# A macaron decoder layer on one core: 512-column products grouped ahead of 256-column ones, and the statistics of two norm boundaries taken another way

## The chip, the core and the metric

The kernel runs on one core of a Trainium2 chip. TensorE multiplies (PE in the rows, with its weight loads as PEld), VectorE (DVE), ScalarE (ACT) and GpSimd (POOL) do the elementwise work, and SyncE (SP) issues nearly all DMAs. The metric is the device time of one execution in microseconds; three executions of the kernel before gave 2088.93, 2089.51 and 2091.53 us, the median being 2089.51.

## The reference

The layer works on 16 meta tokens and 256 tokens (272 in all) of width 2048, in float32:

```
hs = concat(meta, x)                                   # 272 x 2048
f  = swiglu(rms(hs, g1pre), w_gate, w_up, w_down)      # 2048 -> 5632 -> 2048
hs = hs + 0.5 * rms(f, g1post)                         # boundary 1 ...
m  = mixer(rms(hs, g2pre), w_in, ..., w_out)           # ... with this norm
hs = hs + rms(m, g2post)                               # boundary 2 ...
f  = swiglu(rms(hs, g3pre), w_gate2, w_up2, w_down2)   # ... with this norm
out = (hs + 0.5 * rms(f, g3post))[16:]
```

The mixer is one projection by `w_in` (2048 x 7264), two kinds of attention on its parts (top-k attention with an indexer, and gated linear attention), and `w_out` (2048 x 2048). `rms(y, g)` is `y * rsqrt(mean(y*y) + eps) * g`.

## The kernel before, in words

**Products.** Activations lie transposed: 128 features on the partitions, tokens along the free dimension, 16 chunks of 128 features. Each float32 operand is split into an upper part (`hi`, float32r) and the rest (`lo`), and a product is `hi*hi + lo*hi + hi*lo`, summed in PSUM. A weight block of 512 x 512 is loaded by one DMA of 1 MB into a `raw` tile (3 buffers, L110, L220, and L598), and `split` (L103) makes of each half a `whi` tile on ScalarE (L104) and a `wlo` tile on VectorE (L105), 5 buffers each.

**`stream_block` (L144).** One block of 512 output features: 4 units of 512 input features (`u`), in each unit 4 tiles of 128 output features (`f`), and for each of them 4 chunks (`k`). With 272 tokens a chunk takes three products of 272 columns (`mm3`, L137 to L139). With 256 tokens the upper and lower parts of the activation lie side by side, so that a chunk takes one product of 512 columns (`hi` weight by both parts, L192) and one of 256 columns (`lo` weight by the upper part, L193), in turn: 512, 256, 512, 256, and so on. These blocks are 5 blocks of `w_in`, 4 of `w_out`, and 20 of the second gate and up: 29 blocks of 16 times 4 pairs, 1856 pairs. The two halves of the 512 columns are added after it by `joined` (L204: a ScalarE copy of one half, L207, and a VectorE sum, L208).

**`stream_pair` (L210).** Right behind each boundary two blocks run side by side, all in products of 256 columns (L249, L250, L252; at boundary 1 with one more tile of 272 columns): 16 chunks in turn, each with 24 or 27 products. Its weights come as splits numbered `i = 4u + 2j + ...` (L228), four to a unit.

**Operands in SBUF.** `xg` (L275) holds the normed activations of 272 tokens, one chunk to 2 x 272 columns (2176 bytes); `xn2` (L278) is a view of the same tile for 256 tokens, one chunk to 2 x 256 columns (2048 bytes), from its first byte on. `xs2` hands it to `w_out`, and to the second gate and up, as the moving operand.

**The two boundaries.** Boundary 1 lies between the last down projection of the first FFN (`down1`, L570, its last call at L594) and the `w_in` pair; boundary 2 between `w_out` (L1003) and the pair of the second gate and up. Each needs the sum of squares of a whole row before the next stage can start. `square_add` (L337) squares a chunk on ScalarE and adds it on GpSimd, chunk by chunk; the last chunk (15) is squared and added on VectorE (L340, L341). Then `stat_cols` (L292) sums over the partitions on TensorE with a column of ones, `rstd_cols` (L299) makes the reciprocal root (L305 to L310), `Boundary` (L351) spreads it over the partitions with TensorE (`bcast`, L316) and makes the first three chunks of the next stage's activation (`chunk`, L370: VectorE L373 and L376, ScalarE L379 for the upper and VectorE L380 for the lower part); the others follow while `stream_pair` runs. `keep_busy(n)` (L268) puts `n` products of 256 columns with no use for their result into TensorE's queue; the counts stand in `BUSY` (L33): 12 ahead of the statistics, 7 ahead of the spreading, 12 behind it.

**What sets the order.** TensorE's instructions run in the order written. The other engines' order is made by a planner from dependencies and program order; `order(ins, prior)` (L96) tells it to put one instruction behind another on its engine without a wait. `Boundary.how` (L364) puts the splits `i >= 5` of a pair behind chunk 1's upper part on ScalarE; the splits 0 to 4 are free. Behind `down1` (L596 to L604) the kernel loads 96 narrow columns of `w_in` (`small_w`) and splits them, through one of the `raw` buffers.

## Time and profile before

| | |
|---|---|
| three executions | 2088.93, 2089.51, 2091.53 us |
| the profiled execution | 2088.96 us, of which the span from first to last instruction is 2087.2 us |
| TensorE busy | 99% of the span, 13,992 products |
| VectorE, ScalarE, GpSimd busy | 60%, 45%, 2% |
| granted TensorE clock | 0.998 of full speed over the span |
| DMA | 360.72 MB, mean 173 GB/s |

Products are pipelined: the time that the profile gives to one (400 ns for 512 columns) overlaps with that of its neighbours, so the pace is read from the starts of consecutive products. A row of a timeline gives start, duration, engine, line, operation, output and inputs, shape and count.

### The profile page before, as it was taken

The numbers are of one execution on the slowest core, as the hardware profiler recorded it, in microseconds if no ns is written. First come the engines' busy times: TensorE is split into PE (matmuls) and PEld (weight loads), VectorE is DVE, ScalarE is ACT, GpSimd is POOL, SyncE is SP. The second block draws the span as 40 slices with busy tenths as digits, with TensorE's granted clock in tenths as the row PEclk, the third lists the DMA queues.
The fourth block names the chain that finished last, engine by engine and source line by source line (L and its number), as shares of the span: only waits on it lengthen the run. The fifth ranks groups of instructions, "written<-read, shape, count | busy, mean of one in ns | idle before, by whom it ended". The sixth has DMA issues, their size and how long they took to land.

```text
span 2087.2 us, 33405 instructions
## 1 busy us (share of the span) xinstructions
PE 2066.7 (99%) x13992; PEld 1922.0 (92%) x13992; DVE 1260.7 (60%) x1874; ACT 944.2 (45%) x1348; POOL 50.1 (2%) x64
## 2 busy tenths in 40 slices
PE   9999999999999999999999999999999999999998
PEld 9999999999999999989989998898888888888886
DVE  6455555545555557778755454766656565566657
ACT  6333333333343345564544355564444444444443
POOL 3000000000000002000000001100000000000000
PEclk9999999999999999999999999999999999999999
DMA  7555555555555555444443445465655555555653
GB/s 246 172 172 183 168 176 181 166 179 178 168 180 177 168 181 152 151 141 140 161 140 123 159 145 179 145 202 183 196 186 182 193 190 183 191 191 183 198 184 121
DMA packets 184649, 360.72 MB, mean 173 GB/s; under 512 B 9919, under 2 KB 10513, under 8 KB 184354
## 3 DMA queue, kind: packets, MB, share of 16 engines
q1 hardware_dynamic: 183552, 356.41, 52.4%
q8 instruction: 110, 1.80, 0.4%
q10 hardware_dynamic: 786, 2.14, 0.3%
q14 instruction: 41, 0.34, 0.1%
q0 software_dynamic: 160, 0.03, 0.0%
HBM read 356.46 MB, written 2.10 MB: 172 GB/s over the span
## 4 chain that ended last, share of the span: by engine, by line
PE 97%; DVE 2%; ACT 1%; issue 1%; DMA 0%; POOL 0%; SPq 0%; DVEq 0%; ACTq 0%
PE mmb L192 21%; PE mmb L139 15%; PE mmb L137 15%; PE mmb L138 15%; PE mmb L193 10%; PE mmb L1039 4%; PE mmb L1040 4%; PE mmb L1041 4%; PE mmb L249 2%; PE mmb L250 2%; PE mmb L252 2%; PE axb L790 1%; PE axb L855 0%; DVE wlo L105 0%; PE axb L704 0%
## 5 line engine op out<-in xcount | busy, mean ns | idle before, releaser
L105 DVE TENSOR_TENSOR wlo<-raw,whi 128x1024 fp32r<-128x1024 f32 (+1 forms) x674 | 807.1, 1221 | 608.0 <-ACT whi L104 607.9
L104 ACT ACTIVATE whi<-raw 128x1024 fp32r<-128x1024 f32 (+1 forms) x674 | 684.2, 1050 | 809.5 <-PE mmb L139 408.8
L192 PE MATMUL mmb<-xg,whi 128*128 128x512 f32 x1856 | 661.5, 400 | 0.0
L193 PE MATMUL mmb<-xg,wlo 128*128 128x256 f32 x1856 | 521.1, 281 | 0.0
L137 PE MATMUL mmb<-xg,whi 128*128 128x272 f32 x1792 | 520.5, 290 | 0.2 <-DVE qk L631 0.2
L139 PE MATMUL mmb<-xg,whi 128*128 128x272 f32 x1792 | 517.4, 289 | 0.0
L138 PE MATMUL mmb<-xg,wlo 128*128 128x272 f32 x1792 | 514.8, 287 | 0.0
L192 PEld LDWEIGHTS mmb<-xg,whi 128*128 128x128 f32 x1856 | 348.8, 188 | 87.3 <-issue 4.0
L193 PEld LDWEIGHTS mmb<-xg,wlo 128*128 128x128 f32 x1856 | 350.5, 189 | 0.4
L137 PEld LDWEIGHTS mmb<-xg,whi 128*128 128x128 f32 x1792 | 336.6, 188 | 4.9 <-issue 3.6
L139 PEld LDWEIGHTS mmb<-xg,whi 128*128 128x128 f32 x1792 | 337.5, 188 | 0.0
L138 PEld LDWEIGHTS mmb<-xg,wlo 128*128 128x128 f32 x1792 | 336.8, 188 | 0.2
L139 PE MATMUL mmb<-hlo,whi 128*128 128x272 f32 x704 | 204.1, 290 | 0.0
L137 PE MATMUL mmb<-hhi,whi 128*128 128x272 f32 x704 | 203.8, 289 | 0.0
L138 PE MATMUL mmb<-hhi,wlo 128*128 128x272 f32 x704 | 202.1, 287 | 0.0
L1039 PE MATMUL mmb<-whi,hhi 128*128 128x512 f32 (+1 forms) x356 | 138.0, 388 | 0.0
L1041 PE MATMUL mmb<-wlo,hhi 128*128 128x512 f32 (+1 forms) x356 | 137.8, 387 | 0.0
L1040 PE MATMUL mmb<-whi,hlo 128*128 128x512 f32 (+1 forms) x356 | 137.7, 387 | 0.0
L137 PEld LDWEIGHTS mmb<-hhi,whi 128*128 128x128 f32 x704 | 133.1, 189 | 0.0
L139 PEld LDWEIGHTS mmb<-hlo,whi 128*128 128x128 f32 x704 | 132.7, 188 | 0.0
L138 PEld LDWEIGHTS mmb<-hhi,wlo 128*128 128x128 f32 x704 | 132.5, 188 | 0.0
L583 DVE TENSOR_TENSOR acc<-mmb,acc 128x272 f32<-128x272 f32 x160 | 70.0, 439 | 78.0 <-PE mmb L139 78.0
(262 smaller groups left out, 1634.9 us busy)
## 6 DMA issues: line engine op xcount, KB each, us to landing
raw<-in_ffn_w_up_dram SPq DMA_DIRECT2D x88, 1024.0 KB, 5.1
raw<-in_ffn_w_down_dram SPq DMA_DIRECT2D x88, 1024.0 KB, 5.0
raw<-in_ffn_w_gate_dram SPq DMA_DIRECT2D x87, 1024.0 KB, 5.1
raw<-in_w_in_dram SPq DMA_DIRECT2D x56, 1024.0 KB, 5.0
raw<-in_w_out_dram SPq DMA_DIRECT2D x16, 1024.0 KB, 5.0
xn<-in_x_dram SPq DMA_DIRECT2D x3, 512.0 KB, 8.1
raw<-in_ffn_w_gate_dram SPq DMA_DIRECT2D x4, 256.0 KB, 5.1
grep<-in_ffn_post_g_dram ACTq DMA_DIRECT2D x1, 1024.0 KB, 4.9
```

The source lines that it names most:

```text
L104: for ins, prior in zip((act.activation(hi, raw, AF.Copy), eng.tensor_tensor(lo, raw, hi.bitcast(F32), op=ALU.subtract)), after):
L105: eng.tensor_tensor(lo, raw, hi.bitcast(F32), op=ALU.subtract)), after):
L137: pe.matmul(ps, whi, xhi, start=start, stop=False)
L138: pe.matmul(ps, wlo, xhi, start=False, stop=False)
L139: pe.matmul(ps, whi, xlo, start=False, stop=stop)
L192: pe.matmul(wide, hi, both, start=ui == 0 and k == 0, stop=False)
L193: pe.matmul(wide[:, 0], lo, both[:, 0], start=False, stop=ui == 3 and k == 3)
L249: pe.matmul(ps, hi, xh, start=c == 0 and own, stop=False, skip_group_check=True)
L583: dve.tensor_tensor(acc[:, c], ps[:, :T], acc[:, c], op=ALU.add)
L1039: pe.matmul(ps, hh[:, tk], whi, start=k == 0, stop=False)
L1040: pe.matmul(ps, hl[:, tk], whi, start=False, stop=False)
L1041: pe.matmul(ps, hh[:, tk], wlo, start=False, stop=k == 3)
```

## The change

Six things change, and the diff below is cut to them.

- In `stream_block` with 256 tokens, the four products of 512 columns of a tile `f` come first and then its four of 256 columns. A tile named in `plain` takes three products of 256 columns for each chunk instead (`mm3`), so that its sum stands in one half of the bank; this is used for the last tile of `w_out` (4 times 4 chunks), whose result is then copied by VectorE without `joined`.
- `xn2` starts `XOFF = 64` elements (256 bytes) into `xg`.
- Squares are added on VectorE for all chunks (before: GpSimd). Chunk 15's square is made on VectorE (`square_last`) but not added there: `stat_cols2` lets TensorE sum the running sum's columns and then the last square's columns into the same place.
- The idle products at the boundaries: 2 (between the two halves of `stat_cols2`), 5 and 9 in place of 12, 7 and 12.
- In `Boundary.how` the lower part of split 0 goes behind the last square, that of split 1 behind the reciprocal, splits 2 to 4 behind chunk 1's upper part (ScalarE) and lower part (VectorE); from 5 on as before.
- The load and split of `small_w` move ahead of the last `gate_up` of the first FFN.

```diff
-BUSY = (12, 2, 12, 7, 12)
+BUSY = (12, 2, 2, 5, 9)
...
+                    x = [xs(4 * u + k)[:, :, sl] for k in range(4)]
                     for k in range(4):
                         hi, lo = wof(k, f)
-                        both = xs(4 * u + k)[:, :, sl]
-                        pe.matmul(wide, hi, both, start=ui == 0 and k == 0, stop=False)
-                        pe.matmul(wide[:, 0], lo, both[:, 0], start=False, stop=ui == 3 and k == 3)
+                        if f in plain:
+                            mm3(wide[:, 0], hi, lo, x[k][:, 0], x[k][:, 1], ui == 0 and k == 0, ui == 3 and k == 3)
+                        else:
+                            pe.matmul(wide, hi, x[k], start=ui == 0 and k == 0, stop=False)
+                    for k in range(0 if f in plain else 4):
+                        pe.matmul(wide[:, 0], wof(k, f)[1], x[k][:, 0], start=False, stop=ui == 3 and k == 3)
...
-    xn2 = xg.rearrange("p c s t -> p (c s t)")[:, :KC * 2 * NX].rearrange("p (c s t) -> p c s t", c=KC, s=2)
+    xn2 = xg.rearrange("p c s t -> p (c s t)")[:, XOFF:XOFF + KC * 2 * NX]
+    xn2 = xn2.rearrange("p (c s t) -> p c s t", c=KC, s=2)
...
+    def stat_cols2(sq, last, toks):
+
+        ps = ax_bank()
+        for j, s in enumerate((sq, last)):
+            for i, (t0, t1) in enumerate(toks):
+                pe.matmul(ps[:, i:i + 1], s[:, t0:t0 + P], ones, start=j == 0 and i == 0, stop=j == 1,
+                          skip_group_check=True)
+            if j == 0:
+                keep_busy(BUSY[2])
+        return ps[:, 0:len(toks)]
...
+    def square_last(src, n):
+        q = st.tile([P, T], F32, name="sqt", bufs=3)
+        return q, dve.tensor_tensor(q[:, :n], src, src, op=ALU.mult)
...
         def how(self, i):
-            return dict(after=(self.later, None)) if i >= 5 else {}
+            if i < 2:
+                return dict(after=(None, self.behind[i]))
+            return dict(after=(self.later, self.lower if i < 5 else None))
...
     for b in range(NB):
+        if b == NB - 1:
+
+            w_in = a["w_in"]
+            small_w = mixp.tile([P, 2, KC, P], F32R, name="mix")
...
     rr1 = st.tile([P, 3], F32, name="rrc", bufs=2)
-    keep_busy(BUSY[2])
-    rstd_cols(rr1, stat_cols(sq, TOK), D, unscaled=ev1)
+    lastq, last = square_last(acc[:, KC - 1], T)
+    root = rstd_cols(rr1, stat_cols2(sq, lastq, TOK), D, unscaled=ev1)
     keep_busy(BUSY[3])
...
             for f in range(4):
                 c = 4 * j + f
-                joined(mix[:, c], banks[f])
-                square_add(sq, mix[:, c], c == 0, NX, last=c == KC - 1)
+                if c < KC - 1:
+                    joined(mix[:, c], banks[f])
+                    prior = square_add(sq, mix[:, c], c == 0, NX)
+        dve.tensor_copy(mix[:, KC - 1], banks[3][:, :NX])
         rr2 = st.tile([P, 3], F32, name="rrc", bufs=2)
-        keep_busy(BUSY[2])
-        rstd_cols(rr2, stat_cols(sq, TOKX), D)
+        lastq, last = square_last(mix[:, KC - 1], NX)
+        order(last, prior)
+        root = rstd_cols(rr2, stat_cols2(sq, lastq, TOKX), D)
```

## Rows read from the trace of the kernel before

**Rows 1.** From the page: busy time and share of the span of each engine, and the chain that ended last by engine.

```profile
PE 2066.7 (99%) x13992; PEld 1922.0 (92%) x13992; DVE 1260.7 (60%) x1874; ACT 944.2 (45%) x1348; POOL 50.1 (2%) x64
PE 97%; DVE 2%; ACT 1%; issue 1%; DMA 0%; POOL 0%; SPq 0%; DVEq 0%; ACTq 0%
```

**Rows 2.** From the page: the costliest groups of instructions, here the split on VectorE and the 512-column products (count, busy us, mean ns of one, idle before).

```profile
L105 DVE TENSOR_TENSOR wlo<-raw,whi 128x1024 fp32r<-128x1024 f32 (+1 forms) x674 | 807.1, 1221 | 608.0 <-ACT whi L104 607.9
...
L192 PE MATMUL mmb<-xg,whi 128*128 128x512 f32 x1856 | 661.5, 400 | 0.0
```

**Rows 3.** TensorE's timeline in the second FFN: the first product of two blocks of gate and up (128 pairs), the first of the 96 products of 512 columns of the down projection behind them, and the first product behind that.

```profile
1452.33 0.39 PE L192 MATMUL mmb<-xg,whi 128*128 128x512 f32 x1
...
1497.54 0.40 PE L1039 MATMUL mmb<-whi,hhi 128*128 128x512 f32 x1
...
1519.37 0.39 PE L192 MATMUL mmb<-xg,whi 128*128 128x512 f32 x1
```

**Rows 4.** The same timeline: the 5th and the 12th of those 96 products.

```profile
1498.49 0.39 PE L1040 MATMUL mmb<-whi,hlo 128*128 128x512 f32 x1
...
1500.10 0.39 PE L1041 MATMUL mmb<-wlo,hhi 128*128 128x512 f32 x1
```

**Rows 5.** From the chain that ended last, in order of time (start, us, what): the last 8 products of a chunk of the pair behind boundary 2, and those of the chunk 12 chunks later; a chunk is 24 products of 256 columns.

```profile
1340.02 0.96 PE mmb L252 x8
...
1374.58 0.96 PE mmb L252 x8
```

**Rows 6.** TensorE's timeline in the pair behind boundary 1: first and last of 16 products of 256 columns in chunk 1, and of the same 16 in chunk 2.

```profile
824.55 0.29 PE L249 MATMUL mmb<-xg,whi 128*128 128x256 f32 x1
...
826.26 0.28 PE L250 MATMUL mmb<-xg,wlo 128*128 128x256 f32 x1
...
827.70 0.28 PE L249 MATMUL mmb<-xg,whi 128*128 128x256 f32 x1
...
829.47 0.28 PE L250 MATMUL mmb<-xg,wlo 128*128 128x256 f32 x1
```

**Rows 7.** Boundary 1, timeline of TensorE: the last product of the down projection, the statistics, and the first product of the pair.

```profile
811.64 0.29 PE L139 MATMUL mmb<-hlo,whi 128*128 128x272 f32 x1
...
815.82 0.83 PE L296 MATMUL axb<-ones,sq 128*128 128x1 f32 x6 [2.47 <-DVE sq L341]
...
821.00 0.41 PE L249 MATMUL mmb<-xg,whi 128*128 128x256 f32 x1
```

**Rows 8.** Boundary 1, timeline of VectorE and, last, of ScalarE.

```profile
811.96 0.44 DVE L583 TENSOR_TENSOR acc<-mmb,acc 128x272 f32<-128x272 f32 x1 [1.06 <-PE mmb L139]
812.40 1.52 DVE L105 TENSOR_TENSOR wlo<-raw,whi 128x1024 fp32r<-128x1024 f32 x1
813.85 0.43 DVE L340 TENSOR_TENSOR sqt<-acc 128x272 f32<-128x272 f32 x1
814.20 1.21 DVE L105 TENSOR_TENSOR wlo<-raw,whi 128x1024 fp32r<-128x1024 f32 x1
815.34 0.43 DVE L341 TENSOR_TENSOR sq<-sq,sqt 128x272 f32<-128x272 f32 x1
816.69 0.16 DVE L308 SCALAR_TENSOR_TENSOR pv<-axb,ev 128x3 f32<-128x3 f32 x1 [0.92 <-PE axb L296]
817.12 0.18 DVE L310 RECIPROCAL rrc<-sd 128x3 f32<-128x3 f32 x1 [0.27 <-ACT sd L309]
818.67 0.44 DVE L373 TENSOR_TENSOR bu<-acc,axb 128x272 f32<-128x272 f32 x1 [1.38 <-PE axb L321]
...
819.68 0.52 ACT L379 ACTIVATE xg<-hsT,gcol 128x272 fp32r<-128x272 f32 x1 [2.59 <-DVE hsT L376]
```

**Rows 9.** Busy time of each engine in stretches of boundary 1 (window, its length, busy us and count of PE, PEld, DVE, ACT, POOL, then the granted clock, DMA share and GB/s).

```profile
814.00:816.00 2.00, 0.18 (x2) 0.18 (x2) 1.77 (x3) 0.00 (x0) 0.00 (x0) 1.00 0.73 179
...
820.00:822.00 2.00, 2.00 (x12) 2.00 (x12) 1.97 (x5) 1.36 (x4) 0.00 (x0) 0.56 0.03 8
```

**Rows 10.** Boundary 2, timeline of TensorE: the last product of `w_out` and the first of the pair.

```profile
1327.01 0.28 PE L193 MATMUL mmb<-xg,wlo 128*128 128x256 f32 x1
...
1334.97 0.39 PE L249 MATMUL mmb<-xg,whi 128*128 128x256 f32 x1
```

**Rows 11.** Boundary 2, timeline of VectorE, with the ScalarE square of chunk 14 first.

```profile
1327.47 0.40 ACT L346 ACTIVATE sqt<-mix 128x256 f32<-128x256 f32 x1
...
1328.74 0.42 DVE L208 TENSOR_TENSOR mix<-mmb,sqt 128x256 f32<-128x256 f32 x1
1329.12 1.37 DVE L105 TENSOR_TENSOR wlo<-raw,whi 128x1024 fp32r<-128x1024 f32 x1
1330.42 0.41 DVE L340 TENSOR_TENSOR sqt<-mix 128x256 f32<-128x256 f32 x1
1330.93 0.42 DVE L341 TENSOR_TENSOR sq<-sq,sqt 128x256 f32<-128x256 f32 x1
1332.35 0.17 DVE L310 RECIPROCAL rrc<-sd 128x2 f32<-128x2 f32 x1 [0.99 <-ACT sd L305]
1333.43 0.42 DVE L373 TENSOR_TENSOR bu<-mix,axb 128x256 f32<-128x256 f32 x1 [0.92 <-PE axb L321]
```

**Rows 12.** SyncE's issue of the load of `small_w`; and, from the page, the loads of a weight matrix with KB each and median us from issue to landing.

```profile
790.36 1.76 SPq L601 DMA_DIRECT2D raw<-in_w_in_dram  x2
...
raw<-in_ffn_w_up_dram SPq DMA_DIRECT2D x88, 1024.0 KB, 5.1
```

More of the change, by code (lines that the diff above doesn't have):

```diff
@@ L144, in stream_block @@
     def stream_block(w, c0, xs, sl, korder=(0, 1, 2, 3), chunked=False, extra=None, before=None, how=None,
-                     raw=None):
+                     raw=None, plain=()):
         n = sl.stop - sl.start
@@ L309, in rstd_cols @@
             act.activation(q[:, :w], v[:, :w], AF.Sqrt)
-        dve.reciprocal(dst[:, :w], q[:, :w])
+        return dve.reciprocal(dst[:, :w], q[:, :w])
     def eps_var(dst, src, n):
@@ L335, in sqrt_table, with square_add @@
         act.activation(j, after, AF.Sqrt, bias=eps, scale=0.0)
-    def square_add(sq, src, first, n, eng=pool, last=False):
-        if last:
-            q = st.tile([P, T], F32, name="sqt", bufs=3)
-            dve.tensor_tensor(q[:, :n], src, src, op=ALU.mult)
-            dve.tensor_tensor(sq[:, :n], sq[:, :n], q[:, :n], op=ALU.add)
-        elif first:
+    def square_add(sq, src, first, n):
+        if first:
             act.activation(sq[:, :n], src, AF.Square)
@@ L379, in chunk @@
             h = act.activation(hi, hsT[:, c, sl], AF.Copy, scale=gn[:, c:c + 1])
-            dve.scalar_tensor_tensor(lo, hsT[:, c, sl], gn[:, c:c + 1], hi.bitcast(F32),
-                                     op0=ALU.mult, op1=ALU.subtract)
+            i = dve.scalar_tensor_tensor(lo, hsT[:, c, sl], gn[:, c:c + 1], hi.bitcast(F32),
+                                         op0=ALU.mult, op1=ALU.subtract)
             if c == 1:
-                self.later = h
+                self.later, self.lower = h, i
         def __call__(self, ui, k):
@@ L399, in __call__ @@
                 for d in range(c, c + 1) if c < 12 else range(12, KC):
-                    self.last = square_add(self.sq, hsT[:, d, self.sl], d == 0, self.n, dve)
+                    self.last = square_add(self.sq, hsT[:, d, self.sl], d == 0, self.n)
     grow = const.tile([P, P], F32, name="grow")
@@ L583, in down1 @@
                     dve.tensor_tensor(acc[:, c], ps[:, :T], acc[:, c], op=ALU.add)
-                if b == NB - 1:
-                    square_add(sq, acc[:, c], c == 0, T, last=c == KC - 1)
+                if b == NB - 1 and c < KC - 1:
+                    square_add(sq, acc[:, c], c == 0, T)
                 bg.tick(12 * us)
@@ L589, in layer_kernel @@
     for b in range(NB):
+        if b == NB - 1:
+            w_in = a["w_in"]
+            small_w = mixp.tile([P, 2, KC, P], F32R, name="mix")
+            raw = wp.tile([P, KC, P], F32, name="raw", bufs=3)
+            pool.memset(raw[:, :, 64:128], 0.0)
+            for c0, n, o in ((C_IK, 80, 0), (C_GL, 16, 96)):
+                nc.sync.dma_start(out=raw[:, :, o:o + n],
+                                  in_=w_in[:, c0:c0 + n].rearrange("(k p) c -> p k c", p=P))
+            for j in range(2):
+                js = slice(8 * j, 8 * j + 8)
+                split(raw[:, js], small_w[:, 0, js], small_w[:, 1, js])
         hid = gate_up(fp, a["ffn1_w_gate"], a["ffn1_w_up"], b, xs, full, begin.r, first if b == 0 else None)
@@ L594, in layer_kernel @@
     down1(NB - 1, prev)
-    w_in = a["w_in"]
-    small_w = mixp.tile([P, 2, KC, P], F32R, name="mix")
-    raw = wp.tile([P, KC, P], F32, name="raw", bufs=3)
-    pool.memset(raw[:, :, 64:128], 0.0)
-    for c0, n, o in ((C_IK, 80, 0), (C_GL, 16, 96)):
-        nc.sync.dma_start(out=raw[:, :, o:o + n], in_=w_in[:, c0:c0 + n].rearrange("(k p) c -> p k c", p=P))
-    for j in range(2):
-        js = slice(8 * j, 8 * j + 8)
-        split(raw[:, js], small_w[:, 0, js], small_w[:, 1, js])
     rr1 = st.tile([P, 3], F32, name="rrc", bufs=2)
-    keep_busy(BUSY[2])
-    rstd_cols(rr1, stat_cols(sq, TOK), D, unscaled=ev1)
+    lastq, last = square_last(acc[:, KC - 1], T)
+    root = rstd_cols(rr1, stat_cols2(sq, lastq, TOK), D, unscaled=ev1)
     keep_busy(BUSY[3])
-    bound = Boundary(lambda c: acc[:, c], rr1, TOK, full, g1post, g2pre, r2c, None, xs, full)
+    bound = Boundary(lambda c: acc[:, c], rr1, TOK, full, g1post, g2pre, r2c, None, xs, full, (last, root))
     ffn1_ctx.close()
@@ L1004, in layer_kernel @@
         for j in range(4):
-            banks = stream_block(a["w_out"], j * BW, xs2, alone, korder=korder, before=split_mix if j == 0 else None)
+            banks = stream_block(a["w_out"], j * BW, xs2, alone, korder=korder, before=split_mix if j == 0 else None,
+                                 plain=(3,) if j == 3 else ())
             if j == 2:
@@ L1009, in layer_kernel @@
                 c = 4 * j + f
[L1010 to L1011 removed]
+                if c < KC - 1:
+                    joined(mix[:, c], banks[f])
+                    prior = square_add(sq, mix[:, c], c == 0, NX)
+        dve.tensor_copy(mix[:, KC - 1], banks[3][:, :NX])
         rr2 = st.tile([P, 3], F32, name="rrc", bufs=2)
[L1013 to L1014 removed]
+        lastq, last = square_last(mix[:, KC - 1], NX)
+        order(last, prior)
+        root = rstd_cols(rr2, stat_cols2(sq, lastq, TOKX), D)
         keep_busy(BUSY[3])
[L1016 removed]
+        bound = Boundary(lambda c: mix[:, c], rr2, TOKX, xsl, g2post, g3pre, r3c, ev3, xs2, alone,
+                         (last, root))
         first = stream_pair(a["ffn2_w_gate"], 0, a["ffn2_w_up"], 0, xs2, alone, bound, bound.how)
```

8 lines of the change are left out of this document (4 added, 4 removed).

## The prediction

> **What bounds the kernel now.** I read the page's busy shares and its chain by engine first, then TensorE's timeline in a long stretch without stalls, then all engines' timelines at the two boundaries. The first two give the frame: TensorE is busy 99% of the span and makes up 97% of the chain that ended last [rows 1]. So only two things can shorten the time: a closer pace of its products, or less time at the boundaries, where its queue holds idle products that count as busy.
>
> The pace is read from starts. Two blocks of gate and up, 128 pairs, take 1497.54 - 1452.33 = 45.21 us [rows 3], 353.2 ns a pair. Alone, the two kinds are quicker: from the 12th product of the down projection to the next block's first are 85 products of 512 columns in 1519.37 - 1500.10 = 19.27 us [rows 3, 4], 226.7 ns each; and 12 chunks of 24 products of 256 columns take 1374.58 - 1340.02 = 34.56 us [rows 5], 120.0 ns each. Together 346.7, so a pair taken in turn costs 6.5 ns more than its parts. I read that as a price of changing the length, 3.25 ns a change, two changes a pair.
>
> At boundary 1 the next stage's first product starts 821.00 - 811.64 = 9.36 us after the last one of the stage before [rows 7], at boundary 2 1334.97 - 1327.01 = 7.96 us after it [rows 10]. What ends last there is VectorE's queue: two splits of 1.52 and 1.21 us stand between the sum into chunk 15, its square and its addition [rows 8]; at boundary 2 one of 1.37 us [rows 11]. Both belong to the next stage's weights and could wait.
>
> **The change part by part.** The sum is made against the profiled execution: 2088.96 us, 0.55 below the median of 2089.51; it transfers to the median as a difference.
>
> *Products regrouped.* 1856 pairs [rows 2] are 464 groups of four; four of them become `plain`, 460 change. A group costs 4 x 353.2 = 1413 ns now. Regrouped it has four of each kind and two changes in place of eight: 4 x 346.7 + 2 x 3.25 = 1393 ns, 20 ns less; 460 x 20 = 9.2 us. The trace has no such group, so both ends: the good one has all 512-column products at 226.7 and the 256-column ones at the best pace of the trace, (826.26 - 824.55) / 15 = 114.0 ns [rows 6]: 1363 ns, 23 us less. The bad one takes the nearest rows for a few 512-column products right behind 256-column ones, the first four of the down projection: (1498.49 - 1497.54) / 4 = 237.5 ns [rows 3, 4], with 120.0 for the others: 1430 ns, 7.8 us more. I take 9.2, since the long runs stand on 85 and 288 products, and the four slow ones on one place where weights and bank change as well. I apply it to the 80 groups of `w_in` too, for which I show no row.
>
> *The 256 bytes.* The address of the moving operand does matter in this trace: 16 products take 1.71 us between first and last in chunk 1 and 1.77 us in chunk 2 [rows 6], 114 against 118 ns, and what differs is a step of 2176 bytes in `xg`, which is 8.5 times 256. Whether a step of 256 bytes alone does anything, no row shows; if it repeats the pace at a whole number of 256, it does nothing, and that is the nearest reading. I take 0; ends: 6 ns on 768 products of the second pair, 4.6 us either way.
>
> [...]
>
> *`plain`.* Four groups of twelve 256-column products, 1440 ns in place of 1413: 0.1 us in all, and only the last, at most 0.03 us, meets the boundary. It saves ScalarE's copy of chunk 15. VectorE's copy I price as its sum, 0.42 [rows 11].
>
> *Boundary 1.* VectorE goes from the sum (811.96, done 812.40) straight to the square: done 812.83. The addition is TensorE's now, and the earlier chunks' columns are summed before it. From the end of the last addition (815.77) to the next VectorE step (816.69) are 0.92 us [rows 8], so that step could start at 813.75. But split 0's lower part, 1.22 us [rows 2], is now released by the square and fills the gap till 814.05. Then the reciprocal 0.43 later, 814.48. From it to the spread factor 1.55 us [rows 8], of which I cut 0.15 because seven idle products stood in between and there are five: 815.9. Split 1's lower part, behind the reciprocal, ends at 815.9 as well and costs nothing more. Then 1.01 us to the upper part of chunk 0 and its 0.52 [rows 8]: first product at 817.45 in place of 821.00, 3.55 us less. [...] In sum 3.9.
>
> *Boundary 2.* The copy of chunk 15 and chunk 14's addition, now VectorE's (0.42 each), follow the last product: chunk 14's chain had its square at 1327.47 although a split stood ahead of it [rows 11], so that both are done at about 1328.2, and the square at 1328.6. From the start of the addition to the reciprocal were 1332.35 - 1330.93 = 1.42 us [rows 11], 1.0 without the addition: 1329.6, held by split 0 till 1329.85. The factor 1.08 later [rows 11], 1330.93, held by split 1 (from 1330.0) till 1331.25. From there to the first product 1334.97 - 1333.43 = 1.54 [rows 10, 11]: 1332.8, 2.1 us less.
>
> *Additions on VectorE* (14 at each boundary, 0.42 to 0.43 us): hidden, VectorE being busy 60% [rows 1]; without that cover they cost 0.4 us at chunk 14. *`small_w`*, two loads issued at 790.36 [rows 12] and two splits: ahead of the last gate and up they are covered by the unit of weights that lies split in advance; bounds 0 to the 1.8 us of the issue. *Splits 2 to 4* move 3 x 1.22 us behind chunk 1. They hide behind the pair's first two chunks of 2.88 us each [rows 5], but their `raw` buffers come free later: split 2 ends some 3.4 us into the pair of boundary 2, the second matrix of unit 1 lands 5.1 us [rows 12] after that, at 8.5, its two split steps of some 1.2 us end at 10.9, and chunk 4 asks for it at 4 x 2.88 = 11.5. I take 0; bounds 0 and 2 us.
>
> Sum: 9.2 + 3.9 + 2.1 - 0.1 = 15.1 us; 2088.96 becomes 2073.9, and the median **2074.4 us**.
>
> **The rivals.**
> - *The order of the products costs nothing* (the 6.5 ns belong to the weight loads' or the operands' places, and follow them into the new order). For it: each kind alone was measured with other operands and banks. Against it: a change of length is the one thing the mixed stretch has that neither run has. Then only the boundaries remain: 2089.5 - 5.9 = 2083.6.
>
>   [...]
> - *Every product gets quick* (no change of length left to speak of, and the new address hits the good pace): near 1363 ns a group: 2089.5 - 23 - 5.9 = 2060.6; halfway to it 2067.
> - *The products don't settle*: behind a change it takes more than four products to reach the pace of a long run, so that each group of four stays at 237.5, as the first four of the down projection do [rows 3, 4]. Place: every group. Price: 1430 ns, 7.8 us more, against 5.9 less at the boundaries: 2091.4, slower than before. It decides from 13 ns a group on. Against it: the down projection's first products also change bank and weights.
> - *The boundaries give little*: with fewer idle products (16 for 31) the granted clock falls there again, as it did in 820 to 822 [rows 9], or the late weights stall chunk 4. Each boundary then gives back up to 2 us, and the forecast becomes 2078.4.
>
> **How the numbers follow.** Forecast 45%, own range 2069 to 2080; order costs nothing 22%; quick products 15%; boundaries give little 10%; not settling 8%. The range 2063 to 2086 leaves out the best of the quick cases and most of the unsettled ones. What a measurement can tell from no change is about 0.2%, 4.2 us. Faster by more than that: the forecast, the quick and nearly all of the little-boundary cases, and two thirds of the second (its 5.9 is near the limit): 83%. Within: the rest of it and most of the unsettled: 13%. Slower: 4%.
>
> **What would show it.** In the second FFN the 128 pairs of two blocks should take 44.6 us in place of 45.2, with four 512-column starts about 228 ns apart and then four about 120. The first product of the next stage should start 5.8 us after the last one at both boundaries, with square, then split 0, then reciprocal on VectorE, and no window below a granted clock of 1.0. TensorE should not pause in the pairs' first five chunks. Wrong it would be if the blocks stay at 45.2 us, or if the 512-column starts stay at 235 or more.

## The result, and the profile after

Four executions of the changed kernel gave 2077.95 to 2079.53 us, median 2079.49; four of the kernel before, on the same chip, 2088.93 to 2091.68, median 2090.52. The ratio is 0.9946, with a 95% interval of 0.9929 to 0.9963: faster by 0.5%, 5.1 us short of the forecast and inside its range. The profiled execution took 2079.47 us, its span is 2077.5 us (before 2087.2).

The page of the changed kernel, busy times and the chain by engine, answers to [rows 1]:

```profile
PE 2060.6 (99%) x13988; PEld 1920.6 (92%) x13988; DVE 1269.1 (61%) x1900; ACT 942.4 (45%) x1347; POOL 20.6 (1%) x36
PE 95%; issue 2%; DVE 1%; ACT 1%; DMA 0%; POOLq 0%; DVEq 0%; POOL 0%; ACTq 0%
```

TensorE is still 99% busy, so the shares say nothing of where the 9.8 us of span went. The starts of products do. The stages below are cut at the first and last product of each in the two traces; the last column is the best kernel of the experiments.

| stage | before, us | after, us | difference | best, us |
|---|---|---|---|---|
| start to last product of the first FFN | 811.64 | 811.90 | +0.26 | 806.14 |
| boundary 1 | 9.36 | 6.31 | -3.05 | 5.66 |
| pair behind it | 53.18 | 53.04 | -0.14 | 52.94 |
| rest of the mixer | 354.68 | 354.39 | -0.30 | 355.92 |
| `w_out` | 98.14 | 97.68 | -0.46 | 96.56 |
| boundary 2 | 7.97 | 5.27 | -2.70 | 5.34 |
| pair behind it | 47.03 | 47.03 | 0.00 | 46.13 |
| rest of the second FFN | 695.42 | 692.05 | -3.37 | 687.01 |
| tail | 9.83 | 9.83 | 0.00 | 9.84 |

The boundaries gave 5.75 us where 6.0 were forecast. The new order of the products gave 4.1 us in its three stages (rest of the mixer, `w_out`, rest of the second FFN) where 9.2 were forecast: that is where the missing 5 us are. The best kernel's 355.92 us in the mixer hold a fall of TensorE's granted clock at 1108 us; `xoff48`, the same there but for the fall, took 354.37, 1.55 less.

TensorE's timeline in the second FFN, the stretch of [rows 3]: the 128 pairs of two blocks of gate and up, from their first product to the first of the down projection, with the first groups of four kept together as the view merges them.

```profile
1445.70 1.07 PE L197 MATMUL mmb<-xg,whi 128*128 128x512 f32 x4
1446.61 0.64 PE L199 MATMUL mmb<-xg,wlo 128*128 128x256 f32 x4
1447.08 1.09 PE L197 MATMUL mmb<-xg,whi 128*128 128x512 f32 x4
1448.01 0.63 PE L199 MATMUL mmb<-xg,wlo 128*128 128x256 f32 x4
1448.48 1.09 PE L197 MATMUL mmb<-xg,whi 128*128 128x512 f32 x4
...
1490.58 0.40 PE L1066 MATMUL mmb<-whi,hhi 128*128 128x512 f32 x1
```

1490.58 - 1445.70 = 44.88 us; the prediction asked for 44.6, before it was 45.21. A group takes 44.88 / 32 = 1402.5 ns: 10.3 less than before, not 20. The second group shows which part is dear: four products of 512 columns from 1447.08 to 1448.01, 232 ns each and not 228, and four of 256 in 0.47 us, 118 ns each.

Boundary 1, the answer to [rows 7, 8], on VectorE with ScalarE's upper part:

```profile
812.22 0.44 DVE L603 TENSOR_TENSOR acc<-mmb,acc 128x272 f32<-128x272 f32 x1
812.70 0.44 DVE L365 TENSOR_TENSOR sqt<-acc 128x272 f32<-128x272 f32 x1
813.06 1.22 DVE L107 TENSOR_TENSOR wlo<-raw,whi 128x1024 fp32r<-128x1024 f32 x1
814.20 0.15 DVE L326 SCALAR_TENSOR_TENSOR pv<-axb,ev 128x3 f32<-128x3 f32 x1
814.62 0.18 DVE L328 RECIPROCAL rrc<-sd 128x3 f32<-128x3 f32 x1 [0.27 <-ACT sd L327]
814.71 1.20 DVE L107 TENSOR_TENSOR wlo<-raw,whi 128x1024 fp32r<-128x1024 f32 x1
816.53 0.44 DVE L393 TENSOR_TENSOR bu<-acc,axb 128x272 f32<-128x272 f32 x1 [0.62 <-PE axb L339]
...
817.54 0.52 ACT L399 ACTIVATE xg<-hsT,gcol 128x272 fp32r<-128x272 f32 x1 [2.95 <-DVE hsT L396]
```

Square, split 0, reciprocal, split 1 stand in the predicted order and, counted from the sum, within 0.3 us of the predicted times up to the end of split 1. Then VectorE waits 0.62 us for the spread factor (L339), which was forecast to be there. TensorE's timeline and the granted clock (last column but two in the windows, as in [rows 9]) say why:

```profile
813.89 0.84 PE L278 MATMUL mmb<-idle 128*128 128x256 f32 x5
814.94 1.55 PE L339 MATMUL axb<-ident,rrc 16*128 16x16 f32 x6 [0.21 <-DVE rrc L328]
816.14 2.27 PE L278 MATMUL mmb<-idle 128*128 128x256 f32 x9
818.21 0.48 PE L255 MATMUL mmb<-xg,whi 128*128 128x256 f32 x1
```

```profile
812.00:814.00 2.00, 1.98 (x17) 1.77 (x16) 1.89 (x4) 0.00 (x0) 0.00 (x0) 1.00 0.00 0
814.00:816.00 2.00, 1.79 (x11) 1.58 (x11) 1.64 (x4) 0.20 (x1) 0.00 (x0) 0.78 0.00 0
816.00:818.00 2.00, 2.00 (x12) 2.00 (x10) 1.40 (x4) 0.46 (x2) 0.00 (x0) 0.50 0.00 0
818.00:820.00 2.00, 2.00 (x16) 2.00 (x16) 2.00 (x6) 1.96 (x5) 0.00 (x0) 0.86 0.03 8
```

The granted clock fell to 0.50 of full speed (throughout 816 to 818), although TensorE had been busy 1.98 us of the window 812 to 814 and 1.79 us of 814 to 816, in which the clock fell (0.78). The six products that spread the factor took 1.55 us so, and the nine idle products 2.27; in `best`, below, where the clock stayed at 1.00 at this boundary, they took 1.00 and 1.32.

Boundary 2, the answer to [rows 10, 11]:

```profile
1323.32 0.28 PE L141 MATMUL mmb<-xg,whi 128*128 128x256 f32 x1
1323.59 0.43 DVE L361 TENSOR_TENSOR sq<-sq,sqt 128x256 f32<-128x256 f32 x1 [0.48 <-ACT sqt L360]
1323.94 0.42 DVE L1036 COPY mix<-mmb 128x256 f32<-128x256 f32 x1
1324.39 0.42 DVE L365 TENSOR_TENSOR sqt<-mix 128x256 f32<-128x256 f32 x1
1324.73 1.22 DVE L107 TENSOR_TENSOR wlo<-raw,whi 128x1024 fp32r<-128x1024 f32 x1
1325.87 0.16 DVE L328 RECIPROCAL rrc<-sd 128x2 f32<-128x2 f32 x1
1325.94 1.21 DVE L107 TENSOR_TENSOR wlo<-raw,whi 128x1024 fp32r<-128x1024 f32 x1
1327.06 0.42 DVE L393 TENSOR_TENSOR bu<-mix,axb 128x256 f32<-128x256 f32 x1
...
1328.59 0.39 PE L255 MATMUL mmb<-xg,whi 128*128 128x256 f32 x1 [0.74 <-ACT xg L399]
```

The next stage starts 5.27 us after the last product, in place of 7.97. Chunk 14's addition and chunk 15's copy end at 1324.36, 1.04 us after the last product's start; the forecast had 1.2 and, for the square, 1.6 where 1.5 was measured. Both splits are on the path here, but only just: ScalarE's root ends at 1325.77 and the reciprocal behind split 0 starts 0.10 us later; the spread factor ends at 1326.79 and the step behind split 1 starts 0.27 us later.

### The profile page after: what moved, and what is told of

It reads as the page before. It is cut to its first block, busy times and chain, and to the rows that moved or that the text cites. A ratio compares the mean times of both kernels' runs of the same rounds, so it can differ in the third digit from the quotient of the medians.

```text
span 2077.5 us, 33335 instructions
## 1 busy us (share of the span) xinstructions
PE 2060.6 (99%) x13988; PEld 1920.6 (92%) x13988; DVE 1269.1 (61%) x1900; ACT 942.4 (45%) x1347; POOL 20.6 (1%) x36
## 4 chain that ended last, share of the span: by engine, by line
PE 95%; issue 2%; DVE 1%; ACT 1%; DMA 0%; POOLq 0%; DVEq 0%; POOL 0%; ACTq 0%
PE mmb L197 20%; PE mmb L141 15%; PE mmb L139 15%; PE mmb L140 15%; PE mmb L199 10%; PE mmb L1067 4%; PE mmb L1066 4%; PE mmb L1068 4%; PE mmb L255 2%; PE mmb L256 2%; PE mmb L258 2%; PE axb L877 0%; DVE wlo L107 0%; PE axb L812 0%; PE mmb L183 0%
## 5 line engine op out<-in xcount | busy, mean ns | idle before, releaser
L139 PE MATMUL mmb<-xg,whi 128*128 128x272 f32 (+1 forms) x1808 | 525.0, 290 | 0.2 <-DVE qk L653 0.2
L141 PE MATMUL mmb<-xg,whi 128*128 128x272 f32 (+1 forms) x1808 | 522.0, 289 | 0.0
L140 PE MATMUL mmb<-xg,wlo 128*128 128x272 f32 (+1 forms) x1808 | 519.3, 287 | 0.0
L197 PE MATMUL mmb<-xg,whi 128*128 128x512 f32 x1840 | 506.2, 396 | 0.0
L197 PEld LDWEIGHTS mmb<-xg,whi 128*128 128x128 f32 x1840 | 314.9, 189 | 46.5 <-issue 4.0
L139 PEld LDWEIGHTS mmb<-xg,whi 128*128 128x128 f32 x1808 | 339.6, 188 | 4.8 <-issue 3.6
L141 PEld LDWEIGHTS mmb<-xg,whi 128*128 128x128 f32 x1808 | 340.5, 188 | 0.0
L140 PEld LDWEIGHTS mmb<-xg,wlo 128*128 128x128 f32 x1808 | 339.8, 188 | 0.2
L199 PEld LDWEIGHTS mmb<-xg,wlo 128*128 128x128 f32 x1840 | 281.8, 188 | 39.3
L199 PE MATMUL mmb<-xg,wlo 128*128 128x256 f32 x1840 | 292.1, 280 | 0.0
```

The lines of the kernel that those rows point to most:

```text
L139: pe.matmul(ps, whi, xhi, start=start, stop=False)
L140: pe.matmul(ps, wlo, xhi, start=False, stop=False)
L141: pe.matmul(ps, whi, xlo, start=False, stop=stop)
L197: pe.matmul(wide, hi, x[k], start=ui == 0 and k == 0, stop=False)
L199: pe.matmul(wide[:, 0], wof(k, f)[1], x[k][:, 0], start=False, stop=ui == 3 and k == 3)
```

## Experiments

Each kernel is the changed one with the edit shown; times of single executions stand beside 2091.75 to 2092.32 us of the kernel before. Stage times come from the traces as in the table.

**What the new order gives, and what the 256 bytes give.** `alt0` and `alt64` put the products back in turn, with the operand at its old place and 256 bytes on; `xoff0` keeps the groups and puts the operand back.

```diff
 alt0, alt64:
                             pe.matmul(wide, hi, x[k], start=ui == 0 and k == 0, stop=False)
+                            pe.matmul(wide[:, 0], lo, x[k][:, 0], start=False, stop=ui == 3 and k == 3)
-                    for k in range(0 if f in plain else 4):
-                        pe.matmul(wide[:, 0], wof(k, f)[1], x[k][:, 0], start=False, stop=ui == 3 and k == 3)
 alt0, xoff0:
-XOFF = 64
+XOFF = 0
```

> The changed kernel with the products in turn again (512, 256, 512, 256) and the moving operand at its old place: the boundaries alone are left of the change. All theories: the pairs of gate and up back at 1412.8 ns a group of four pairs, span about 2077.5 + 460 x 10.3 ns = 2082.2 us, that is 5 us below the kernel before; the two boundaries as in the changed kernel, 6.3 and 5.3 us from the last product to the first.

> The changed kernel with the products in turn again, but the moving operand still 256 bytes on. Theory order (the new order alone brings the closer pace): 1412.8 ns a group, span about 2082.2 us. Rival address (the 256 bytes bring it, or part of it): below 1410 ns a group, 1402.5 if all of it, span then 2077.5 us.

> The changed kernel with the moving operand at its old place, products grouped. Theory order (256 bytes are a whole period and do nothing): 1402.5 ns a group and a span of 2077.5 us as in the changed kernel, the pair behind boundary 2 at 2.88 us a chunk. Rival address: the group goes back towards 1412.8 ns and the span towards 2082.2 us.

Measured: 2087.38 us (`alt0`), 2084.10 (`alt64`), 2077.92 (`xoff0`). A group takes 1412.8 ns in turn with either place, as before, and 1402.5 ns in groups with either place. So the 256 bytes do nothing, and the order gives 10.3 ns a group: 3.37 us in the second FFN and 0.57 in `w_out` between `alt64` and the changed kernel. Most of the rest of the difference in time between these runs goes with the clock: it fell at 908 and 1117 us in `alt0` and at 1114 in `alt64`, inside the mixer, which took 3.39 and 1.84 us more (the mean granted clock is 0.996 in `alt0`, and 0.998 in `alt64`, `xoff0` and the changed kernel). Of that the order can be some 0.3 us: so much the mixer gained by it from the kernel before to the changed one, where the clock fell in neither mixer (1.00 from 870 to 1300 us in both). In `alt64` and `xoff0` the clock did not fall at boundary 1, and that took 5.67 and 5.66 us.

**What a change of length costs.** `group8` and `group16` join two and four tiles: 8 products of 512 columns and 8 of 256, or 16 and 16 (G is 2 and 4).

```diff
+                for f0 in range(0, nf, G):
+                    for f in range(f0, f0 + G):
+                        for k in range(4):
...
+                                pe.matmul(wides[f], hi, x[k], start=ui == 0 and k == 0, stop=False)
+                    for f in range(f0, f0 + G):
+                        for k in range(0 if f in plain else 4):
+                            pe.matmul(wides[f][:, 0], wof(k, f)[1], x[k][:, 0], start=False, stop=ui == 3 and k == 3)
```

> The changed kernel with groups twice as long: eight products of 512 columns (two tiles f), then eight of 256. Theory price (each change of length costs a fixed sum; 1402.5 ns a group of four pairs against 4 x 346.7 for the long runs gives 7.9 ns a change): half the changes, 1394.7 ns for four pairs, span 3.6 us below the changed kernel. Rival settling (what a 512-column product costs behind 256-column ones falls to the long-run 226.7 ns only over about ten products, as at the head of the down projection): 512-column products still at 231 to 234 ns, 1400 to 1406 ns for four pairs, span within 1 us of the changed kernel.

> Sixteen products of 512 columns (a whole unit), then sixteen of 256. Theory price: 1390.8 ns for four pairs. Rival settling: the last products of each sixteen come near 226.7 ns, 1392 to 1400 ns for four pairs, and the 512-column starts draw together within the sixteen. If both fall, and all 512-column products stay at 233 ns whatever the group's length, then it isn't the change of length that they pay for in these stretches.

Four pairs take 1395.8 ns in `group8` and 1390.8 in `group16`, on the way to the 1386.8 of the two kinds alone. One price of 7.9 ns a change, worked out from the changed kernel as (1402.5 - 1386.8) / 2, puts `group8` at 1394.7 and `group16` at 1390.8. But it is not paid at the change. TensorE's timeline of `group8`, one group of eight cut into its first five and last three products of 512 columns:

```profile
1463.43 1.32 PE L198 MATMUL mmb<-xg,whi 128*128 128x512 f32 x5
1464.59 0.84 PE L198 MATMUL mmb<-xg,whi 128*128 128x512 f32 x3
1465.27 1.11 PE L201 MATMUL mmb<-xg,wlo 128*128 128x256 f32 x8
1466.22 0.40 PE L198 MATMUL mmb<-xg,whi 128*128 128x512 f32 x1
```

The first five come (1464.59 - 1463.43) / 5 = 232 ns apart, the other three 0.68 / 3 = 227, the pace of the long run. Over all such groups of the second FFN's long stretches the starts behind a change are 232.9, 235.2, 228.2, 232.1 and 230.6 ns apart, then 226.7 from the sixth on, and in `group16` the same five are slow and the eleven behind them at 226.7. The products of 256 columns go the other way, 113.3 and 119.2 and then 120.0. So the price is real, but in these two runs it is spread over five 512-column products, and a group of four ends before that: its four starts in the changed kernel are 233.9, 234.4, 231.8 and 228.4 ns apart. In turn, where each product is the first behind a change, `alt64` has 236.4 and 116.9.

Both kernels lost as wholes, 2086.75 and 2089.18 us: the second FFN was 1.40 and 2.97 us shorter, but boundary 2 took 2.31 and 4.58 us more, `w_out` 0.90 and 4.53, the mixer 6.89 and 5.59. At boundary 2 the last square starts 2.06 and 3.57 us after the last product's start, in place of 1.07, since the results of two or four tiles are still to be joined, squared and added there; the clock fell at that boundary as well in both. In the mixer it fell once in both (the mean over the run is 0.996 in both, against 0.998 in the changed kernel); how much of the mixer's loss is that and how much the longer groups was not told apart.

**Whether the place of an operand can matter at all.** `xoff48` moves the operand 192 bytes in place of 256.

```diff
-XOFF = 64
+XOFF = 48
```

> The changed kernel with the moving operand 192 bytes on in place of 256. Theory address (what a product costs beyond its columns hangs on where its moving operand lies against the next weights, with a period of 256 bytes; in the pair behind boundary 1 the quick chunks are those whose operand starts 192 bytes past the weights' phase): the 256-column products of the second pair at 114 ns in place of 120, a chunk of 2.74 us in place of 2.88, the pair 2.2 us shorter, and the groups of four below 1390 ns, span at or below 2070 us. Rival (only order counts, the quick chunks are quick for another reason): 2.88 us a chunk, 1402 ns a group, span 2077.5 us.

Measured: 2072.15 us. TensorE's timeline of `xoff48`, first product of the same 128 pairs and first behind them:

```profile
1443.13 0.39 PE L197 MATMUL mmb<-xg,whi 128*128 128x512 f32 x1
...
1487.51 0.39 PE L1066 MATMUL mmb<-whi,hhi 128*128 128x512 f32 x1
```

44.38 us, 1387.0 ns a group, 15.5 less than with 256 bytes. The first of four 256-column products takes 118.4 ns to the next start and the others 113.3, on average 114.6 in place of 118.5. That is the whole gain: the 512-column products take 232.1 ns on average with either place. In the compiled kernels up to here the weight tiles all start at the same place modulo 256 bytes, and in the trace of before the 256-column products behind each other sort by the distance of their moving operand from the weights: 119.6, 118.2 and 119.5 ns at 0, 64 and 128 bytes, 113.5 at 192. That is what 114 against 118 ns in [rows 6] was.

**Whether it holds for 272 and 512 columns.** `ph192` is `xoff48` with the hidden activations of both down projections in padded tiles, so that moving operand and weights stand 192 bytes apart there too. (In the second FFN's down projection `whi` and `wlo` are the moving operands, and the activations take the weights' part.)

```diff
-XOFF = 64
+XOFF = 48
...
-            hi = pool_.tile([P, n], F32R, name="hhi", bufs=8)
-            lo = pool_.tile([P, n], F32R, name="hlo", bufs=8)
+            o = 16 if n == T else 16
+            hi = pool_.tile([P, 320], F32R, name="hhi", bufs=8)[:, o:o + n]
+            lo = pool_.tile([P, 320], F32R, name="hlo", bufs=8)[:, o:o + n]
```

> The changed kernel with the moving operand 192 bytes on (as xoff48) and, besides, the gate-times-up results of both FFNs in tiles of 1280 bytes, placed so that in both down projections, too, every moving operand starts 192 bytes past the phase of the next weights (modulo 256 bytes). Theory address: the 272-column products of the first down projection from a mean of 125.8 to about 123.3 ns, the 512-column ones of the second from 226.7 to about 220 ns, together (2112 x 2.5 + 1056 x 6.7 ns) 12 us below xoff48, span about 2058 us. Rival (the pace of 512 and 272 columns doesn't hang on the address as that of 256 columns does): span within 2 us of xoff48's 2070.2 us.

Measured: 2073.06 us. The first FFN gained 5.5 us against `xoff48`, its 272-column products coming 123.3 ns apart in place of 126.1 on average; but the second FFN lost 6.8. Its down projection there, two products 56 places apart:

```profile
1424.77 0.39 PE L1067 MATMUL mmb<-whi,hhi 128*128 128x512 f32 x1
...
1437.83 0.39 PE L1069 MATMUL mmb<-wlo,hhi 128*128 128x512 f32 x1
```

13.06 / 56 = 233.2 ns, against 226.7 in [rows 3, 4]. In the steady runs of one length measured here 192 bytes are thus the best of the four distances for 256 and 272 columns (113.5 and 123.3 ns) and a bad one for 512 (233.2). In groups of four at 192 bytes the 512-column products take 226.0, 235.8, 230.9 and 235.8 ns: no more on average than at 256 bytes, where the pace of a long run isn't reached either (231.8 to 234.4 for the first three, 228.4 for the fourth).

**Whether each length can have its own distance.** `phase2` moves the `wlo` tiles by 64 bytes, with a filler tile, so that the 512-column products (next weights mostly `whi`) stand at 0 and the 256-column ones (next mostly `wlo`) at 192. It is the only kernel here in which `whi` and `wlo` do not start at the same place modulo 256 bytes.

```diff
-XOFF = 64
+XOFF = 0
...
+    wp.tile([P, 16], F32, name="gap", bufs=1)
...
+            oh, ol = (0, 0) if n == T else (48, 48)
+            hi = pool_.tile([P, 320], F32R, name="hhi", bufs=8)[:, oh:oh + n]
+            lo = pool_.tile([P, 320], F32R, name="hlo", bufs=8)[:, ol:ol + n]
```

> The changed kernel with the moving operand at its old place (as xoff0), all lower weight tiles 64 bytes further on by a filler tile, and the first FFN's gate-times-up tiles as in ph192, the second's set so that two of three products of the second down projection keep their old phase. So in the grouped blocks the 512-column products start at phase 0 against the next (upper) weights, and the 256-column ones at phase 192 against the next (lower) ones. Theory two phases (256-column products want 192, 114 ns for 120, as xoff48 showed; 512-column ones want 0, 226.7 ns for 233, as ph192 showed in the second down projection, 6.8 us longer): 4 x 226.7 + 4 x 114 + 16 = 1379 ns a group at most, 512-column starts at 228 to 231 ns and 256-column ones at 114 to 116; pair behind boundary 2 some 46.5 us; first down projections 5.3 us shorter as in ph192; span about 2064 us, 6 below xoff48. Rival (512-column products in short groups stay at 231 to 234 ns whatever the phase, since the change of length sets them): 1387 ns or more a group, span 2067 us or more.

Measured: 2078.89 us, a miss. A group took 1399.7 ns, its 256-column products 117.7, and the second FFN's down products 232, against 226.7 with all weights at one place. In the first FFN's down projection two kinds of product stood at 192 bytes from the next weights: the one whose own weights start at the same place as the next came at 122.6 ns, the one whose own start 64 bytes off at 131.5. So the distance to the next weights is not the rule. The distance to both weights isn't either: three of the four 256-column products of a group stood at 192 bytes from their own weights and from the next ones, and came at 117.7 ns, not 115.1 as the same three do in `xoff48`; two of the three kinds in the second FFN's down projection stood at 0 from both, and came at 232 ns, not 226.7, beside a third kind at 64. TensorE's timeline of `phase2`, four 256-column products and the next group's first ones:

```profile
1442.30 0.64 PE L203 MATMUL mmb<-xg,wlo 128*128 128x256 f32 x4
1442.77 1.09 PE L201 MATMUL mmb<-xg,whi 128*128 128x512 f32 x4
```

A rival is the moving operand's own place modulo 256 bytes, whatever the weights': it would fit the 256-column products, whose own place in `phase2` is not that of `xoff48`. It does not fit 512 columns, since in the second FFN's down projection of `ph192` the moving `whi` and `wlo` stayed and only the other operand moved, nor the 272-column products above, all at one own place and 122.6 to 131.5 ns apart. I have no rule for `whi` and `wlo` at different places.

**The splits, and the last addition.** `splitsfree` puts back `Boundary.how`; `addback` has VectorE add chunk 15's square again and the statistics in one piece, the idle counts as changed.

```diff
 splitsfree:
-            if i < 2:
-                return dict(after=(None, self.behind[i]))
-            return dict(after=(self.later, self.lower if i < 5 else None))
+            return dict(after=(self.later, None)) if i >= 5 else {}
 addback, in stat_cols2:
...
+        n = toks[-1][1]
+        dve.tensor_tensor(sq[:, :n], sq[:, :n], last[:, :n], op=ALU.add)
+        keep_busy(BUSY[2])
+        return stat_cols(sq, toks)
```

> The changed kernel with the splits' order undone (0 to 4 free again, from 5 on behind chunk 1's upper part). Theory splits (most of what the boundaries gained is that splits no longer stand ahead of the last chunk's sum and square on VectorE): boundary 1 back to between 8.0 and 9.0 us from the last product to the first, boundary 2 to between 6.5 and 7.5, span 3 to 4 us above the changed kernel. Rival additions (the addition on TensorE, the plain last tile and fewer idle products bring it): both boundaries within 0.6 us of 6.3 and 5.3 us.

> The changed kernel with the last square added to the sum on VectorE again, and the column sums behind it in one piece, with two idle products ahead. Theory additions: 0.45 to 0.9 us more at each boundary (one VectorE step of 0.42 and its hand-over, and the products of the sum's columns, 0.3 to 0.4 us, now in the path): 6.1 to 7.2 us at boundary 1 (5.66 without, 6.3 with a lower granted clock, in the changed kernels so far) and 5.7 to 6.2 at boundary 2 (5.27). Rival (the gap is filled by the split that stands behind the square, so that the addition costs nothing): within 0.2 us of 5.66 or 6.3, and of 5.27.

Measured: 2084.32 us (`splitsfree`) and 2087.84 (`addback`). With the splits free boundary 1 takes 7.48 us and boundary 2 6.53, 1.2 and 1.3 more; the first is less than was expected. The sum into chunk 15 and its square have a split between them again, on VectorE's timeline of `splitsfree`:

```profile
812.45 0.44 DVE L601 TENSOR_TENSOR acc<-mmb,acc 128x272 f32<-128x272 f32 x1
812.88 1.22 DVE L107 TENSOR_TENSOR wlo<-raw,whi 128x1024 fp32r<-128x1024 f32 x1
814.03 0.43 DVE L365 TENSOR_TENSOR sqt<-acc 128x272 f32<-128x272 f32 x1
```

With the addition back the boundaries take 8.20 and 6.69 us, 1.9 and 1.4 more, both above what was expected. VectorE's timeline at boundary 1 of `addback`:

```profile
812.94 0.44 DVE L361 TENSOR_TENSOR sqt<-acc 128x272 f32<-128x272 f32 x1
813.30 1.22 DVE L107 TENSOR_TENSOR wlo<-raw,whi 128x1024 fp32r<-128x1024 f32 x1
814.43 0.43 DVE L309 TENSOR_TENSOR sq<-sq,sqt 128x272 f32<-128x272 f32 x1
815.79 0.16 DVE L322 SCALAR_TENSOR_TENSOR pv<-axb,ev 128x3 f32<-128x3 f32 x1 [0.92 <-PE axb L303]
```

The addition itself is 0.43 us, but it stands behind the split that the square releases, and TensorE's sum only starts after it: from square to `pv` 2.85 us in place of 1.50. TensorE pauses 2.26 us before the statistics there. The rest of both kernels' loss goes with the clock again: it fell at both boundaries and in the mixer in both, in `addback` twice in the mixer (the mean over the run is 0.996 in `splitsfree` and 0.994 in `addback`). In the changed kernel it did not fall at boundary 2 (1.00 from 1320 to 1332 us), so what the edits cost there holds some of it.

**The best version, and whether the price of a change remains at 192 bytes.** `best` is `xoff48` with the padding in the first FFN alone; `alt48` is `xoff48` with the products in turn.

```diff
 best:
-XOFF = 64
+XOFF = 48
...
+            o, m = (16, 320) if n == T else (0, n)
+            hi = pool_.tile([P, m], F32R, name="hhi", bufs=8)[:, o:o + n]
+            lo = pool_.tile([P, m], F32R, name="hlo", bufs=8)[:, o:o + n]
```

> The second norm's operand 192 bytes on, and the operands of the first FFN's down projection alone 64 bytes further (padded tiles); the second FFN's stay where they are. Theory (a product's pace hangs on the distance of its moving operand from the next weights, best at 192 bytes for 272 columns and worst there for 512): the first FFN's down products keep 123.3 ns, 5.3 us less than in the kernel with 192 bytes alone, and the second FFN's down products stay at 226.8 ns; span 2070.2 - 5.3 = 2064.9, time about 2066.8, up to 1.5 less where the clock does not fall at boundary 1. Rival (padding the tiles moved other operands too, which cost the 6.8 us in the second FFN): the down products there come at 233 ns again and the time stays at 2072 or more.

> The second norm's operand 192 bytes on, but products of 512 and 256 columns in turn as before. Theory (a change of length has a price of its own, 3.2 ns in turn): a group of four pairs 1387 + 8 x 3.2 = 1412 ns or a little under, the four blocks of 128 pairs in the second FFN's 45.2 us, time about 2080. Rival (the price of a change exists only at the old distance of 0 bytes; at 192 every product is already as slow or as quick as it gets, 233 and 114): 1387 ns in turn as in groups, 44.4 us for 128 pairs, and the time that of the grouped kernel at 192 bytes, 2072 to 2075.

Measured: `best` 2066.74 us (2065.81 to 2067.51, four runs) against 2089.35 (eight runs), ratio 0.9886, interval 0.9870 to 0.9903; that is 0.6% below the changed kernel by the two ratios, and the intervals do not overlap. The second FFN's down products stayed at 226.8 ns and the first FFN's at 123.3, as the theory had it. At its boundary 1 the clock did not fall (1.00 from 806 to 820 us; it did once in the mixer), and the sequence came out as forecast:

```profile
806.14 0.28 PE L141 MATMUL mmb<-hlo,whi 128*128 128x272 f32 x1
...
809.18 1.00 PE L339 MATMUL axb<-ident,rrc 16*128 16x16 f32 x6 [0.22 <-DVE rrc L328]
...
811.81 0.39 PE L255 MATMUL mmb<-xg,whi 128*128 128x256 f32 x1 [0.55 <-ACT xg L399]
```

`alt48` took 2082.12 us (ratio 0.9962, interval 0.9946 to 0.9978) and 1413.2 ns a group, 235.0 and 118.3 ns a product: in turn the pace is that of the old place, so the gain of the 192 bytes exists only with the products in groups, and there a group gains 26.2 ns from the order. The rival, no price at 192 bytes, fell.

## Why the prediction came out as it did

*Products regrouped: wrong in size, and this is nearly all of the error.* The failed step is "Regrouped it has four of each kind and two changes in place of eight: 4 x 346.7 + 2 x 3.25 = 1393 ns". Measured were 1402.5. The 3.25 ns are an average over a stream in which every product stands behind a change. In groups the price is about 7.9 ns a change, and it is spread over the five 512-column products behind it, less what the first two of 256 columns win. A stream in turn breaks this off after one product of each kind, so its average can't show the price of a single change. The three stages gave 4.1 us in place of 9.2. At 10.3 ns the 460 groups would have given 4.7; the 80 groups of `w_in`, for which the prediction had no row, gave 0.3 us and not 0.8, and that stays open.

*The rival "the products don't settle" had the mechanism.* Groups of four do stay among the five slow starts of `group8`; its sign failed by its price, 237.5 ns, where the four average 232.1 and the 256-column products beside them get 1.5 ns quicker. I had set aside the first four of the down projection because weights and bank change there too. But [rows 4] held more: from the 5th to the 12th product are 1500.10 - 1498.49 = 1.61 us for seven, 230 ns each, so the pace had not settled after four. In that trace the first ten products of the down projections are uneven (224 to 241 ns on average) and from the 11th on they come 226.7 ns apart.

*The order does cost something*, so the rival in which it costs nothing fell with `alt64` and `xoff0`; *every product quick* fell with 1402.5 against 1363.

*The 256 bytes: right,* 0 by `alt0` against `alt64` and `xoff0` against the changed kernel. The reason held as well: a shift by 256 bytes leaves the pace (1412.8 ns a group in turn and 1402.5 in groups with either place), and another distance does act: at 192 bytes the 256-column products of a group went from 118.5 to 114.6 ns. The end of 4.6 us counted 768 products; the pair has 16 chunks of 24, that is 384, and the end is 2.3 us. It also left out the groups, where `xoff48` gained most.

*Boundary 1: right in its parts, 3.05 us in this run where 3.9 were forecast.* The sum of 3.9 holds 0.35 us beside the 3.55 of the steps, a term that no run shows. What the runs showed in its place: in the changed kernel the clock fell there (0.50 in 816 to 818) although the pause of 2.47 us [rows 7] was gone. Without the fall the boundary took 5.66 or 5.67 us in eight other kernels of this study, a gain of 3.7 where 3.9 were forecast; with it 5.86 (`alt0`), 6.25 (`xoff48`) and 6.31. It fell at this place in `xoff48` and not in `xoff0`, whose boundary has the same instructions, so the new sequence doesn't prevent it, and what decides was not found. Undoing the two edits costs 1.2 us (order of the splits) and 1.9 us (addition) at this boundary, each with the clock down as in the changed kernel.

*Boundary 2: 2.70 in place of 2.1.* The steps up to the square were priced within 0.2 us. Most of the surplus lies behind it: from the square's start to the reciprocal 1.48 us where 1.65 was forecast, and from split 1's start to the next step 1.12 in place of 1.25, with 1.53 to the first product as forecast; the split's recorded 1.22 us overlaps the next instruction by some 0.1 each time.

*Nothing from `plain`, the additions and the moved load: right within what the start of a run varies* (810.6 to 812.4 us to the first FFN's last product in the kernels whose first FFN is the same). *Splits 2 to 4: right*, the pair behind boundary 2 took 47.03 us before and after.

## What to carry to other kernels

Read the price of a change of shape from runs of several lengths, not from a stream that changes at every step, because the cost can lie in the products behind the change, as here in the first five of 512 columns (228.2 to 235.2 ns, then 226.7). When an instruction is taken off a critical chain, look at what its engine will put into its place: here the addition of 0.43 us cost 1.35, because a split slipped in ahead of it. Where products of a fixed shape come at two paces in one trace, as the 256-column ones here at 113.5 and at 118 to 120 ns, sort them by the places of their operands in SBUF before you believe in noise.

## What was not expected of the hardware

- In the kernels here in which `whi` and `wlo` start at the same place, a product's pace in a run of one length went with where its moving operand starts against its weights (counted modulo 256 bytes, since a shift by 256 left 1412.8 and 1402.5 ns a group as they were), and the good distance differed with the length: 256 columns 113.5 ns at 192 bytes and 118 to 120 at 0, 64 and 128; 272 columns 123.3 at 192 in `ph192`, and in gate and up of the trace of before 122.8 at 192 against 125.2, 128.5 and 125.9 at 0, 64 and 128; 512 columns 226.7 at 0 and 233 at 192. `phase2` shows that the distance alone is not the rule: there 256 columns took 117.7 ns at 192 from their own and the next weights (115.1 in `xoff48`), and 512 columns 232 at 0.
- Behind a change from 256 to 512 columns five products were slow in `group8` and `group16` before the pace of a long run was reached (232.9 ns for the first, 226.7 from the sixth on), at a distance of 0 bytes. At 192 bytes, in groups of four, I can't say which part of the 226.0, 235.8, 230.9 and 235.8 ns is the change.
- The granted clock fell at the same boundary in some kernels (to 0.50 in the changed kernel) and not in others with the same instructions there (1.00 in `best`), and in some also in the mixer; a fall cost some 0.7 us at boundary 1 (6.31 and 53.04 us with the pair behind it, 5.66 and 52.95 in `xoff0`) and some 1.5 us in the mixer (355.92 in `best`, 354.37 in `xoff48`). The pair behind boundary 2 took 45.57 us in `xoff48` and 46.13 in `best` and `alt48`, with the same operands; that stays open.
